# A hybrid diffusion trunk on one core: the output projection takes its weight tiles from the MLP's larger set, and the input's squares take the tiles of split weights

## The chip, the cores and the metric

One NeuronCore of one Trainium2 chip runs the whole kernel. The metric is the device time of one execution in microseconds (us). The engines are TensorE (PE, with its weight loads, PEld), VectorE (DVE), ScalarE (ACT), GpSimd (POOL) and SyncE (SP, which here only issues DMAs). Each works through its own queue in order.

## What is computed

The reference, cut down to what matters here (one layer, 512 latent positions, 256 context positions, model width 2048, MLP width 8192):

```python
mod_l = silu(c) @ w_ada + b_ada                  # 6 x 2048 values: shift, scale, gate, twice
mod_c = silu(c_ctx) @ w_ada + b_ada
p_l = modulate(rms_norm(x, g_mix), sh1_l, sc1_l) @ w_in
p_c = modulate(rms_norm(ctx, g_mix), sh1_c, sc1_c) @ w_in
f_l = fourier_mix(p_l[..., :512], w_fourier)
y_l = ssd_mixer(p_c[..., 512:], p_l[..., 512:], ...)
x = x + gt1_l * (concat([f_l, y_l]) @ w_out)     # the output projection
x = x + gt2_l * (square(relu(modulate(rms_norm(x, g_mlp), sh2_l, sc2_l) @ w_mlp1)) @ w_mlp2)
return rms_norm(x, g_final)
```

## The kernel before

Everything is float32 and lies transposed: channels on the 128 partitions, positions along the free axis, 16 tiles of 128 channels for a width of 2048. Most products split both operands into two parts, `hi` (rounded to the fp32r type by ACT) and `lo` (the remainder, by DVE), and add three matmuls (`mm3`, L106 to L109). `load_split` (L92) loads one weight tile of up to 128 x 1024 through the SP queue into a raw tile `wraw`, makes `whi` on ACT (L100) and `wlo` on DVE (L101), all inside `tc.high_priority()`.

The tiles come from pools with a fixed number of buffers per name. The set that the first half uses (opened at L228) has 3 raw tiles (`wp`) and 2 of each split tile (`ws`). A second set, for the MLP, is opened at L761 with 7 raw tiles and 3 of each split tile; the dictionary `pools` says which set is in use. Instructions are put in order at compile time by a planner: each engine's queue is filled by priority and by the planner's own idea of when inputs and buffers are ready, and this order is fixed when the kernel runs. An instruction that waits holds all that stand behind it in its engine's queue.

**The start.** `spread` (L176) loads the condition vector, one row at a time, into an `araw` tile and spreads it over the partitions by matmuls on `ones` (L183); there is one for the latent condition `cl` and, after the norm of the input, one for the context condition `ccl`. The input `xr` comes in eight loads of two channel tiles each (L317). Its squares (L322, ACT, 128 x 1024 each) go into eight `araw` tiles and are added up by DVE (L324); two matmuls (L328) sum over the channels, and `rstd_of` makes the inverse root (L154 to L159). `araw` has 5 buffers. The same 5 take the 512 KB tiles of `w_ada` (`ada_half`, L169), from which DVE makes the modulation by one multiply-and-sum for each (L173). The first 16 steps of the input projection (L335 to L353) each need four such sums: DVE forms `xr * rstd` (L344), ACT modulates it (`mtmp`, L345), and PE makes eight fp32 products (L349).

**The output projection.** Column block j of 16 has its weights in `w_o[j]`, 1 MB. For j = 0 to 2 the products over the first 13 channel tiles stand ahead of the last SSD results (L743 to L751), and the last three follow in the loop (L797, 192 KB each). From j = 3 on `product` (L111) makes a block of two `load_split` of 512 KB, 24 matmuls of 512 columns each. The sum `ps` (one of 3 `acc` banks) is gated and added to the input tile `x2` by DVE (L803), stored to DRAM by a POOL DMA (L804) and squared for the next norm (L784, L785). `background(3)` puts three `ada_half` steps behind each block: 48 loads of 512 KB for the modulation of the MLP.

**The entry of the MLP.** After the norm (L789, L154 to L159), x is read back, modulated and split into `chi`, `clo` (L837 to L861), and the first MLP weights `w_1s` are loaded by `load_split` in 16 tiles of 384 KB (L848).

Of the kernel before, what the change touches and what calls it, by code (L numbers as in the profile page):

```python
# [7 lines left out]
F32 = mybir.dt.float32  # L8
F32R = mybir.dt.float32r
AF = mybir.ActivationFunctionType  # L10
# [4 lines left out]
P = 128  # L15
D = 2048
KT = D // P
L = 512
# [11 lines left out]
HALF = 1024  # L30
# [25 lines left out]
def tile_hybrid_trunk(ctx, tc, xT, ctxT, cvec, ccol, vec, alog, w_ada, w_adr, w_ins, w_zs, w_in, w_dt, w_f, w_o,  # L56
                      w_1s, w_1, w_2, cst, sel_d, dft, cw_d, out):
    nc = tc.nc
    v = nc.vector
    s = nc.scalar  # L60
    te = nc.tensor
# [7 lines left out]
    pools = {}  # L69
# [5 lines left out]
    def acc(n=L):  # L75
        return psa.tile([P, L], F32, name="acc")[:, :n]

    def bank():
        return psb.tile([P, 512], F32, name="bank")
# [12 lines left out]
    def load_split(src, n, b=None):  # L92

        with tc.high_priority():
            raw = raw_tile()[:, :n]
            hi = pools["ws"].tile([P, HALF], F32R, name="whi")[:, :n]
            lo = pools["ws"].tile([P, HALF], F32R, name="wlo")[:, :n]
            rv = raw if b is None else raw.rearrange("p (a b) -> p a b", b=b)
            nc.sync.dma_start(out=rv, in_=src)
            s.copy(hi, raw)  # L100
            v.tensor_sub(lo, raw, hi.bitcast(F32))  # L101
        if b is None:
            return hi, lo
        return hi.rearrange("p (a b) -> p a b", b=b), lo.rearrange("p (a b) -> p a b", b=b)

    def mm3(ps, a, b, first, last, on=False):  # L106
        te.matmul(ps, a[0], b[0], start=first, stop=False, skip_group_check=on)  # L107
        te.matmul(ps, a[1], b[0], start=False, stop=False, skip_group_check=on)  # L108
        te.matmul(ps, a[0], b[1], start=False, stop=last, skip_group_check=on)  # L109

    def product(ps, src, x, cuts=(8, 16)):  # L111
        k0 = 0
        nk = len(x)
        for k1 in cuts:
            w = load_split(src[:, k0:k1], (k1 - k0) * src.shape[2], src.shape[2])
            for k in range(k0, k1):
                mm3(ps, (w[0][:, k - k0], w[1][:, k - k0]), x[k], k == 0, k == nk - 1)
            k0 = k1
# [8 lines left out]
    ones = const.tile([P, P], F32, name="ones")  # L127
# [99 lines left out]
    w_stack = ExitStack()  # L227
# [3 lines left out]
    ara = ada_stack.enter_context(tc.tile_pool(name="ara", bufs=5))  # L231
# [47 lines left out]
    def background(n):  # L279
        for _ in range(min(n, len(todo))):  # L280
            todo.pop(0)()
# [16 lines left out]
    with tc.tile_pool(name="st", bufs=1, side="right") as st, tc.tile_pool(name="st2", bufs=2, side="right") as st2, \  # L298
            tc.tile_pool(name="st4", bufs=3, side="right") as st4:
        cl = st.tile([P, 2 * HALF], F32, name="cl")  # L300
        xr = st.tile([P, KT, L], F32, name="xr")
# [14 lines left out]
            sl = slice(h * 2, h * 2 + 2)  # L316
            nc.sync.dma_start(out=xr[:, sl], in_=xT[:, sl])  # L317
        s.activation(cs, cs, AF.Silu)
        qs = None
        for h in range(8):  # L320
            q = ara.tile([P, HALF], F32, name="araw")
            s.activation(q, xr[:, h * 2:h * 2 + 2].rearrange("p a b -> p (a b)"), AF.Square)  # L322
            if qs is not None:
                v.tensor_add(q, qs, q)  # L324
            qs = q
        ps = bank()
        for h in range(2):
            te.matmul(ps, ones, qs[:, h * L:(h + 1) * L], start=h == 0, stop=h == 1)  # L328
        rstd = st.tile([P, L], F32, name="rstd")
        rstd_of(rstd, ps, L, 1.0 / D, st2, ("sq", "sr"))  # L330
        spread(ccl, 1)
# [221 lines left out]
    ps = acc(LC)[:48]  # L553
    product(ps, w_dt, cm)
    dt_finish(ps, LC, NCH, cp, ("cxs", "cx_tok"))
    for g in range(NG):
        b_tok = cp.tile([P, NCC, P], F32, name="cb_tok")
        x_tok = cp.tile([P, NCC, HG * 64], F32, name="cx_tok")
        for i in range(4):
            t = T_B + g if i == 0 else T_X + g * 3 + i - 1  # L560
            ps = acc(LC)
# [5 lines left out]
        for d in range(2):  # L567
# [8 lines left out]
            h = cp.tile([P, HG, 64], F32, name="ch")  # L576
# [166 lines left out]
    for j in range(3):  # L743
        ps = acc()
# [14 lines left out]
    new = {}  # L759
# [19 lines left out]
    def sumsq(accum, x, pool, k):  # L779
        if k == 0:  # L780
            s.activation(accum, x, AF.Square)
        else:
            q = pool.tile([P, L], F32, name="nq")
            s.activation(q, x, AF.Square)  # L784
            v.tensor_add(accum, accum, q)  # L785
# [6 lines left out]
    for j in range(KT):  # L792
        x2 = g2p.tile([P, L], F32, name="x2")
        nc.sync.dma_start(out=x2, in_=xT[:, j])
        if j < 3:
            ps = first[j]
            w = load_split(w_o[j][:, 13:16], 3 * P, P)  # L797
            for k in range(13, KT):
                mm3(ps, (w[0][:, k - 13], w[1][:, k - 13]), cat[k], False, k == KT - 1)
        else:  # L800
            ps = acc()
            product(ps, w_o[j], cat)
        v.scalar_tensor_tensor(x2, ps, mod[:, 32 + j:33 + j], x2, ALU.mult, ALU.add)  # L803
        nc.gpsimd.dma_start(out=x2_d[j], in_=x2)  # L804
        sumsq(a1, x2, xp2, j)
        background((21 - NSB) // 2)
    v.scalar_tensor_tensor(s1, mod[:, 64:80], 1.0, vt[:, V_GMLP:V_GMLP + KT], ALU.add, ALU.mult)
    g2_stack.close()
    w_stack.close()
    big_stack.close()  # L810
    pools.update(new)

# [17 lines left out]
    for p in range(8):  # L832
        i, q = p // QC, p % QC
        xa = pr.tile([P, 8, LC], F32, name="xa")
        for k, sl in ((p + 8, slice(1, 3)), (p, slice(0, 4, 3))):
            x = xp2.tile([P, L], F32, name="nt")
# [88 lines left out]
    for rr in range(N1P, NP):  # L925
        ct = stg.tile([P, 4, LC], F32, name="ct")
        sn = stg.tile([P, 4, LC], F32, name="sn")
        ps = {}
# [100 lines left out]
    for c in range(NFC):  # L1029
# [15 lines left out]
        for op in range(4):  # L1045
# [53 lines left out]
            for o in range(2):  # L1099
                for i in range(2):  # L1100
                    j = 2 * op + o + 8 * i
# [9 lines left out]
    ps = bank()  # L1111
# [94 lines left out]
```

## Time and profile before

| what | value |
|---|---|
| median of 3 runs | 2326.96 us (2325.39 to 2330.8) |
| the profiled execution's own time | 2328.78 us |
| its span, first to last instruction | 2327.0 us |
| PE busy | 2235.5 us, 96% of the span |
| DVE busy | 1902.4 us, 82% |
| mean granted TensorE clock | 0.988 of full speed |
| moved by DMA | 499.33 MB |

The profiled execution is one more execution, 1.8 us above the median. In the views, L12 is line 12 of the kernel before. A row of the timeline gives start, duration, engine, line, operation, output<-input and, in brackets, how long the engine had been idle and what ended it. A row of the windows gives, for each engine, busy time (and instructions), then the granted TensorE clock, the mean busy share of the 16 DMA engines and GB/s. Matmuls are pipelined, so their busy times overlap and starts are the better measure.

### The profile page before, as it was taken

How to read it: one execution, taken by the hardware profiler on the slowest of the kernel's cores; microseconds unless marked ns; L12 is line 12 of the kernel's file. 1: busy time of each engine (PE TensorE's matmuls, PEld its weight loads, DVE VectorE, ACT ScalarE, POOL GpSimd, SP SyncE). 2: the span in 40 equal slices, each digit the busy share in tenths (PEclk: the TensorE clock that was granted, in tenths of full speed). 3: DMA queues.
4: the chain of work that ended last, by engine and by line, in shares of the span. 5: the costliest groups of instructions: out<-in, count | busy, mean ns of one | idle time of the engine just before them, and what ended most of it. 6: DMA issues, size and time to landing. Idle time of an engine off the chain costs nothing.

```text
span 2327.0 us, 38787 instructions
## 1 busy us (share of the span) xinstructions
PE 2235.5 (96%) x15218; PEld 1992.7 (86%) x15218; DVE 1902.4 (82%) x2615; ACT 1190.4 (51%) x1706; POOL 319.7 (14%) x346
## 2 busy tenths in 40 slices
PE   6999999999999999799999999999999999999996
PEld 2347779877777777699999999999999999999996
DVE  7977879988889767677888887777997897788788
ACT  4135235456666522255455555555765666566554
POOL 0000000000001000111122121111122222222210
PEclk9999999999999999999999999999999999999998
DMA  7988967743324599546555554344899999999983
GB/s 291 336 313 279 334 235 262 266 145 111 98 88 141 180 316 317 182 136 208 174 180 185 179 167 130 124 131 136 240 265 269 268 255 256 270 268 231 245 261 109
DMA packets 150942, 499.33 MB, mean 215 GB/s; under 512 B 17780, under 2 KB 18692, under 8 KB 150504
## 3 DMA queue, kind: packets, MB, share of 16 engines
q1 hardware_dynamic: 111464, 387.39, 49.1%
q0 software_dynamic: 38144, 107.38, 20.4%
q8 instruction: 119, 1.95, 0.3%
q10 hardware_dynamic: 1152, 2.10, 0.2%
q14 instruction: 63, 0.52, 0.1%
HBM read 433.87 MB, written 62.92 MB: 213 GB/s over the span
## 4 chain that ended last, share of the span: by engine, by line
PE 66%; DVE 15%; DMA 12%; issue 4%; ACT 2%; SPq 0%; POOL 0%; DVEq 0%; ACTq 0%; POOLq 0%
PE acc L108 10%; PE acc L109 10%; PE acc L107 10%; PE bank L107 8%; PE bank L108 8%; PE bank L109 8%; DMA araw<-in_w_ada_dram 3%; DVE wlo L86 2%; DVE araw L173 2%; DMA wraw<-in_w_dram 2%; DVE wlo L101 2%; DMA araw<-in_w_adr_dram 2%; DMA wraw<-in_w_adr_dram 1%; PE bank L349 1%; DVE adacc L201 1%
## 5 line engine op out<-in xcount | busy, mean ns | idle before, releaser
L86 DVE TENSOR_TENSOR wlo<-wraw,whi 128x1024 fp32r<-128x1024 f32 x427 | 552.1, 1301 | 161.1 <-ACT whi L85 158.1
L85 ACT CAST whi<-wraw 128x1024 fp32r<-128x1024 f32 x427 | 444.9, 1048 | 440.0 <-PE bank L109 167.9
L107 PE MATMUL bank<-chi,whi 128*128 128x256 f32 (+1 forms) x2000 | 570.4, 285 | 4.4 <-DVE x2f L1094 2.5
L108 PE MATMUL bank<-chi,wlo 128*128 128x256 f32 (+1 forms) x2000 | 570.2, 285 | 2.5 <-DVE wlo L86 2.5
L109 PE MATMUL bank<-clo,whi 128*128 128x256 f32 (+1 forms) x2000 | 569.8, 285 | 0.0
L107 PE MATMUL acc<-chi,whi 128*128 128x256 f32 (+1 forms) x1512 | 430.9, 286 | 6.7 <-ACT chi L843 6.7
L108 PE MATMUL acc<-chi,wlo 128*128 128x256 f32 (+1 forms) x1512 | 432.8, 286 | 4.6 <-DVE wlo L86 4.3
L109 PE MATMUL acc<-clo,whi 128*128 128x256 f32 (+1 forms) x1512 | 431.0, 285 | 0.0
L107 PEld LDWEIGHTS bank<-chi,whi 128*128 128x128 f32 x2000 | 385.3, 193 | 6.0 <-DVE x2f L1094 2.7
L108 PEld LDWEIGHTS bank<-chi,wlo 128*128 128x128 f32 x2000 | 385.4, 193 | 3.9 <-DVE wlo L86 2.9
L109 PEld LDWEIGHTS bank<-clo,whi 128*128 128x128 f32 x2000 | 385.3, 193 | 1.0
L107 PEld LDWEIGHTS acc<-chi,whi 128*128 128x128 f32 x1512 | 290.0, 192 | 9.2 <-ACT chi L843 7.5
L108 PEld LDWEIGHTS acc<-chi,wlo 128*128 128x128 f32 x1512 | 290.4, 192 | 8.4 <-DVE wlo L86 6.8
L108 PE MATMUL acc<-bh,wlo 128*128 128x512 f32 x720 | 285.8, 397 | 9.9 <-DVE wlo L101 9.9
L109 PEld LDWEIGHTS acc<-clo,whi 128*128 128x128 f32 x1512 | 290.3, 192 | 1.7 <-DVE clo L845 0.6
L107 PE MATMUL acc<-bh,whi 128*128 128x512 f32 x720 | 285.8, 397 | 5.7 <-DVE x L803 3.1
L109 PE MATMUL acc<-bl,whi 128*128 128x512 f32 x720 | 285.0, 396 | 0.0
L100 ACT CAST whi<-wraw 128x1024 fp32r<-128x1024 f32 (+3 forms) x145 | 142.8, 987 | 241.3 <-PE acc L109 207.4
L101 DVE TENSOR_TENSOR wlo<-wraw,whi 128x1024 fp32r<-128x1024 f32 (+3 forms) x145 | 165.7, 1145 | 34.3 <-ACT whi L100 34.0
L108 PEld LDWEIGHTS acc<-bh,wlo 128*128 128x128 f32 x720 | 136.3, 189 | 43.7 <-DVE wlo L101 15.8
L107 PEld LDWEIGHTS acc<-bh,whi 128*128 128x128 f32 x720 | 136.4, 189 | 35.5 <-issue 4.4
L109 PEld LDWEIGHTS acc<-bl,whi 128*128 128x128 f32 x720 | 136.4, 189 | 28.6 <-issue 1.0
(349 smaller groups left out, 3329.7 us busy)
## 6 DMA issues: line engine op xcount, KB each, us to landing
wraw<-in_w_dram SPq DMA_DIRECT2D x276, 512.0 KB, 4.8
araw<-in_w_ada_dram SPq DMA_DIRECT2D x164, 512.0 KB, 6.8
wraw<-in_w_in_dram SPq DMA_DIRECT2D x84, 512.0 KB, 4.5
wraw<-in_w_dram POOLq DMA_DIRECT2D x64, 512.0 KB, 8.0
x<-ca POOLq DMA_DIRECT2D x112, 256.0 KB, 8.2
araw<-in_w_adr_dram SPq DMA_DIRECT2D x48, 512.0 KB, 4.4
wraw<-in_w_adr_dram SPq DMA_DIRECT2D x32, 512.0 KB, 3.9
hid<-ct POOLq DMA_DIRECT2D x32, 512.0 KB, 5.0
```

The costliest lines, as they stand in the source:

```text
L85: s.copy(hi, raw)
L86: v.tensor_sub(lo, raw, hi.bitcast(F32))
L100: s.copy(hi, raw)
L101: v.tensor_sub(lo, raw, hi.bitcast(F32))
L107: te.matmul(ps, a[0], b[0], start=first, stop=False, skip_group_check=on)
L108: te.matmul(ps, a[1], b[0], start=False, stop=False, skip_group_check=on)
L109: te.matmul(ps, a[0], b[1], start=False, stop=last, skip_group_check=on)
L173: v.tensor_tensor_reduce(o, a, cond[:, hf * HALF:(hf + 1) * HALF], 1.0, last if hf else first, ALU.mult, ALU.add, dst[:, ch:ch + 1] if hf ...
L201: v.scalar_tensor_tensor(a, w[:, j], cs[:, k:k + 1], a, ALU.mult, ALU.add)
L349: te.matmul(a[:n], w[:, o:o + n], tmp, start=k == 0, stop=k == KT - 1)
```

## The change

At the start the squares of the input leave the `araw` tiles. They are made in four pairs in the tiles `whi` and `wlo` of the first weight set (2 buffers each): ACT squares the first of a pair, DVE multiplies the second with itself and adds the two, and PE sums each pair by two matmuls at once, so that there are eight matmuls in one sum where there were two. In the output projection the first weight set is closed at j = 3, not behind the loop, and `pools` is switched to the MLP's set there, so that the 26 `load_split` of the blocks j = 3 to 15 take the 7 raw and 3 split tiles.

```diff
-        qs = None
-        for h in range(8):
-            q = ara.tile([P, HALF], F32, name="araw")
-            s.activation(q, xr[:, h * 2:h * 2 + 2].rearrange("p a b -> p (a b)"), AF.Square)
-            if qs is not None:
-                v.tensor_add(q, qs, q)
-            qs = q
         ps = bank()
-        for h in range(2):
-            te.matmul(ps, ones, qs[:, h * L:(h + 1) * L], start=h == 0, stop=h == 1)
+        for h in range(0, 8, 2):
+            q = [pools["ws"].tile([P, HALF], F32R, name=n).bitcast(F32) for n in ("whi", "wlo")]
+            x = [xr[:, i * 2:i * 2 + 2].rearrange("p a b -> p (a b)") for i in (h, h + 1)]
+            s.activation(q[0], x[0], AF.Square)
+            v.tensor_mul(q[1], x[1], x[1])
+            v.tensor_add(q[0], q[0], q[1])
+            for j in range(2):
+                te.matmul(ps, ones, q[0][:, j * L:(j + 1) * L], start=h == 0 and j == 0, stop=h == 6 and j == 1)
...
         else:
+            if j == 3:
+                w_stack.close()
+                pools.update(new)
             ps = acc()
             product(ps, w_o[j], cat)
...
     g2_stack.close()
-    w_stack.close()
     big_stack.close()
-    pools.update(new)
```

## Rows read from the trace of the kernel before

**Rows 1.** The page: busy time of each engine.

```profile
PE 2235.5 (96%) x15218; PEld 1992.7 (86%) x15218; DVE 1902.4 (82%) x2615; ACT 1190.4 (51%) x1706; POOL 319.7 (14%) x346
```

**Rows 2.** Windows, the start of the kernel.

```profile
18.00:20.00 2.00, 0.05 (x1) 0.05 (x1) 1.79 (x2) 0.00 (x0) 0.00 (x0) 1.00 0.12 31
...
40.00:95.00 55.00, 53.93 (x120) 20.00 (x118) 55.00 (x100) 9.64 (x14) 0.00 (x0) 1.00 0.92 327
```

**Rows 3.** Timeline, 0 to 45 us, in order of start.

```profile
3.05 7.16 PE L183 MATMUL bank<-araw,ones 1*128 1x512 f32 x8 [3.05 <-DMA araw<-in_cvec_dram]
...
10.12 1.22 DVE L324 TENSOR_TENSOR araw<-araw 128x1024 f32<-128x1024 f32 x1 [9.11 <-ACT araw L322]
...
10.75 5.78 ACT L322 ACTIVATE araw<-xr 128x1024 f32<-128x1024 f32 x6
...
18.59 12.42 SPq L169 DMA_DIRECT2D araw<-in_w_ada_dram  x8
...
19.95 3.78 PE L328 MATMUL bank<-araw,ones 128*128 128x512 f32 x4 [9.73 <-DVE araw L324]
...
23.66 4.03 PE L183 MATMUL bank<-araw,ones 1*128 1x512 f32 x8
...
28.77 0.69 DVE L159 SCALAR_TENSOR_TENSOR rstd<-sr,rstd 128x512 f32<-128x512 f32 x1
...
32.59 0.08 DVE L173 DVE_READ_ACCUMULATOR2_ANT mod<- 128x1 f32 x1
...
33.57 5.04 PE L349 MATMUL acc<-mtmp,wraw 128*128 128x512 f32 x6 [5.88 <-ACT mtmp L345]
```

**Rows 4.** Timeline of PE, input projection: the first matmuls of four steps.

```profile
80.09 2.84 PE L349 MATMUL acc<-mtmp,wraw 128*128 128x512 f32 x6 [0.45 <-ACT mtmp L345]
...
88.00 2.84 PE L349 MATMUL acc<-mtmp,wraw 128*128 128x512 f32 x6 [0.45 <-ACT mtmp L345]
...
103.20 2.77 PE L349 MATMUL acc<-mtmp,wraw 128*128 128x512 f32 x6
...
110.43 2.77 PE L349 MATMUL acc<-mtmp,wraw 128*128 128x512 f32 x6
```

**Rows 5.** Windows, output projection.

```profile
805.00:810.00 5.00, 1.91 (x7) 1.16 (x6) 4.45 (x7) 3.22 (x5) 0.00 (x0) 0.94 1.03 413
810.00:815.00 5.00, 5.00 (x18) 3.89 (x17) 3.21 (x5) 1.91 (x3) 0.55 (x1) 0.72 0.89 291
...
830.00:835.00 5.00, 5.00 (x17) 3.93 (x16) 2.30 (x4) 0.00 (x0) 0.00 (x0) 0.67 0.88 272
...
830.00:950.00 120.00, 112.82 (x480) 90.04 (x479) 87.45 (x124) 26.94 (x31) 5.93 (x11) 0.99 0.92 316
...
957.00:972.00 15.00, 14.46 (x63) 11.31 (x61) 5.87 (x10) 1.68 (x2) 0.54 (x1) 1.00 0.05 19
```

**Rows 6.** Waits of PE, 797 to 979 us (total, times, longest).

```profile
PE acc L108 <- DVE wlo L101: 8.0, 10, 2.8
PE acc L107 <- DVE x L803: 3.1, 1, 3.1
PE acc L107 <- ACT whi L100: 2.5, 1, 2.5
```

**Rows 7.** DMA issues, 797 to 830 us (KB each, median us to landing).

```profile
wraw<-in_w_1s_dram SPq DMA_DIRECT2D x10, 384.0 KB, 7.5
```

**Rows 8.** Timelines of ACT and of DVE, head of the output projection.

```profile
805.63 3.25 ACT L100 CAST whi<-wraw 128x768 fp32r<-128x768 f32 x5 [5.23 <-DMA wraw<-in_w_1s_dram]
...
806.49 3.63 DVE L101 TENSOR_TENSOR wlo<-wraw,whi 128x768 fp32r<-128x768 f32 x5 [0.55 <-ACT whi L100]
```

**Rows 9.** Timelines of DVE and PE, end of the output projection.

```profile
971.73 0.75 DVE L803 SCALAR_TENSOR_TENSOR x<-acc,mod,x 128x512 f32<-128x512 f32 x1 [8.51 <-PE acc L109]
...
981.75 0.80 PE L107 MATMUL acc<-chi,whi 128*128 128x512 f32 x1 [6.69 <-ACT chi L843]
```

**Rows 10.** Windows, entry of the MLP.

```profile
982.00:1020.00 38.00, 38.00 (x225) 33.70 (x226) 37.59 (x63) 26.37 (x38) 6.01 (x11) 0.94 0.52 161
```

## The prediction

> **What bounds the kernel now.** I read the page first: PE is busy for 96% of the span, so time can only come from places where PE waits or runs at a low clock [rows 1]. I then took windows and timeline of the two stages that the edits touch. In both the DMA share is 0.92 over long stretches [rows 2, 5]. For the output projection I added the waits of PE and the DMA issues.
>
> In the start PE does nearly nothing until its first product of the input projection at 33.57 us; from there it is almost never idle. That product waits for `mtmp`, and `mtmp` waits for the fourth sum over `w_ada` (L173, done at 32.67), though the norm was ready at 28.77 + 0.69 = 29.46 [rows 3]. The sums are late because the loads of `w_ada` are first issued at 18.59, when the squares leave `araw` tiles; between 18 and 20 us DMA runs at 0.12 [rows 2, 3]. Later, from 40 to 95 us, DVE is busy for all of 55 us and PE's steps come 7.91 us apart (80.09 to 88.00), where later, with DVE ahead, they come 7.23 apart (103.20 to 110.43) [rows 2, 4].
>
> In the output projection PE has an average of 112.82 / 480 = 0.235 us for a matmul, so a half block of 24 is worth 5.6 us and a block 11.3 us; DMA moves 316 GB/s at a share of 0.92 [rows 5]. Between 797 and 972 us PE waits 8.0 us for `wlo`, 3.1 for L803 to empty a bank and 2.5 for `whi` [rows 6]. After the two longer gaps the granted clock reads 0.72 and 0.67 in five-microsecond windows, stretches that mix the 1.2 GHz level with 2.4 GHz, which cost 5 x 0.28 + 5 x 0.33 = 3.0 us [rows 5]. All of it together, 13.6 + 3.0 = 16.6 us, is the most that this stage can give. Part of the cause stands in rows 7: ten loads of `w_1s`, which nobody needs before 981 us, go out before 830 us, because the MLP's tiles stand empty and the loads have high priority. They are 10 x 0.393 = 3.93 MB, 12.4 us at 316 GB/s, in a stage whose DMA is nearly full, while from 957 to 972 us DMA lies at 0.05 [rows 5, 7]. ACT's and DVE's casts of them stand in front of those that PE waits for: ACT waits 5.23 us for their DMA [rows 8].
>
> **The change, part by part. The start.** Removed: four of eight squares on ACT and three of seven adds. Added on DVE: four multiplies and, for seven adds, four: eight operations of 1.22 us, 9.8 us, in place of 8.5 [rows 3]; DVE has nothing else before 25 us, so this is hidden by its idle time, and would cost 1.3 us if DVE had the sums to do then. Added on PE: six matmuls, twelve passes. A pass took 7.16 / 8 = 0.895 to 3.78 / 4 = 0.945 us before 24 us, and 0.50 as a mean of the eight from 23.66 [rows 3].
>
> When is the sum of squares ready? The last square ran until 16.53, so the last part of x was there at about 15.5; one multiply and one add give 17.9, two matmuls at the slow pace 21.7, against 23.73 now, so 2 us earlier. But two split tiles of a name make a ring: the third pair waits until PE has read the first, and PE is with the spread of `cl` until 10.2. Sixteen passes from there at 0.895 end at 24.5, 0.8 later than now; at 0.50 for the last pairs it would be near 19.8, 3.9 earlier. And if the planner puts the eight matmuls of the second spread, whose rows no longer wait for `araw`, ahead of the last pairs, it is up to 7.2 later. I take no change of the norm (it lies between the ring and the free chain), with ends of -3.9 and +8.0.
>
> The Trainium skill, "TensorE: Matmul & The Clock Gate", Part 1, has the throttled clock as the default, which activity releases. By it the added matmuls would bring the fast pace earlier and the norm 3.9 us earlier; the eight matmuls from 3.05 to 10.2 us, slow to the last, do not bear that out.
>
> What does come earlier is `w_ada`: `araw` is free while x lands, so about three loads go out behind x and two more follow as the rows of the spread leave. Their sums fall into DVE's idle time and no longer hold `mtmp`. Then the first product follows the norm by the multiply L344 and `mtmp`; the latter took 0.9 us from 32.67 to 33.57, the former is an operation of the 0.69 us of L159, and with latencies I estimate 1.9 us: 31.3 instead of 33.57, -2.3 us. DVE also enters the long stretch some five sums ahead, so that the 7.91 - 7.23 = 0.7 us lost in each of some four steps go: 2.7 at most, of which I take -2.2. Sum of the start: -4.5. Bounds: -3.9 - 2.3 - 2.2 = -8.4, and +8.0 - 2.3 = +5.7 with nothing won in the steps.
>
> **The output projection.** The 26 tiles of blocks 3 to 15 now come before `w_1s` in the ring of seven. So `w_1s` can't be loaded ahead of the stage; in its place at the head go seven half blocks that the stage needs anyway. A `w_1s` load waits until a tile that lies seven before it has been split, which puts the first near nine half blocks, 50 us, before PE's end and the last of seven near 17. PE can be three split tiles deep instead of two: DVE may be 11 us late, not 5.6, before PE waits. With blocks of 2 x 0.524 MB of weights, 3 x 0.524 of `w_ada`, 0.26 in and 0.26 out, 3.15 MB in 11.3 us, PE asks for 279 GB/s, less than the 316 that DMA gave, so PE should be the limit. I count 7.0 of the 8.0 us for `wlo`, the 3.1 for L803 and 2.4 of the 3.0 of clock as won: -12.5. The 2.5 us at the head stay, since the first half blocks take the place that `w_1s` has in the queues of SP, ACT and DVE, with 512 KB instead of 384. Bounds: -16.6, all of it; and, if DMA decides by bytes alone, only the three loads of `w_1s` beyond the seven leave the stage: 1.18 MB, -3.7. Closing the first set issues nothing.
>
> **The entry of the MLP.** Now three tiles of `w_1s` are split by 810 us. After the change two are by the end of PE's work, and the third is made beside the norm. Between 982 and 1020 us DVE is busy 37.59 of 38 us [rows 10], so a split that falls there is paid in full: the five in rows 8, three of 768 columns and two of 384, take 3.63 us, so 0.9 for 768. One is +1; all three are +2.7. Their loads are hidden behind the 10 us from 971.73 to 981.75 in which PE waits for the norm and `chi` [rows 9].
>
> Sum: -4.5 - 12.5 + 1.0 = -16.0 us, from 2328.78 to 2312.8. The median of the runs is 1.8 below the profiled time, so I state 2311. What can't be told from no change is 0.2%, 4.7 us.
>
> **The rivals.** (1) Forecast, both edits pay: 2311, own range 2302 to 2318. Chance 0.52.
>
> (2) DMA is the limit in the output projection. For it: share 0.92, and DVE's waits for `w_ada` are what makes `wlo` late. Against it: 279 below 316 GB/s. Then -3.7 - 4.5 + 1 = -7.2: 2320. Chance 0.18.
>
> (3) The ring of two split tiles and the second spread make the norm late: the start at +5.7, the rest as forecast: -5.8, 2321. For it: slow passes until 24 us. Against: the second spread has lower priority. Chance 0.12.
>
> (4) Nothing much: waits change their names, DVE's order is still paced by `w_ada` landing: 2325 to 2329. Chance 0.10.
>
> (5) Slower: the burst at the head. Seven loads of 512 KB, 3.67 MB, are 8.9 us at the 413 GB/s of 805 to 810 us [rows 5]; if the 192 KB tiles of blocks 1 and 2 and the `x` tiles of L794 stand behind all of them on SP, PE's wait of 2.5 us grows by 6.4, that for L803 by as much, and with DMA the limit only 3.7 comes back: +12.8 - 3.7 + 2.7 - 4.5 = +7.3, 2334. It decides once the head loses more than 3.7 - 2.7 + 4.5 + 4.7 = 10 us. For it: `w_1s` in the same place held ACT for 5.23 us [rows 8]. Against: the first 192 KB tiles need no new set and go first. Chance 0.08. The Trainium skill, "DMA: Bandwidth & Descriptors", Queues, rings and completion order, says that descriptors of one row are consumed in ring order, so what SP issues later waits for the burst; by that rule this rival gets its full price.
>
> **The numbers.** Faster 0.80 (1, 2 and nearly all of 3), same 0.12, slower 0.08. The range leaves out rival 5, most of 4 and a little below the forecast: 2302 to 2326.
>
> **What would show it.** First L173 before 20 us and first L349 near 31; steps 7.2 us apart from the second on. No `w_1s` load before 900 us; PE's wait for `wlo` under 2 us; L803 of the last block near 955 instead of 971.73, with the norm and `chi` some 10 us behind it as now. Wrong, if DMA stays full to the end of the stage, if PE's first wait grows past 10 us, or if the eight matmuls end after 25 us.

## The result and the profile after

The kernel after takes 2312.35 us in the median of 5 runs (2309.25 to 2319.66), the kernel before on the same chip 2330.8 us (2325.39 to 2335.89). The ratio is 0.9935, with an interval of 0.9918 to 0.9951: 11 to 19 us less, where 16 were forecast. The profiled execution took 2314.14 us, its span is 2312.4 us against 2327.0. One execution, of the run with the switch at j = 4, took 3169.61 us at a mean granted clock of 0.637 and is left out of that run's ratio.

In the page, PE's busy time has hardly moved [rows 1], so over the whole span the 14.6 us came out of PE's idle time (91.5 us before, 75.1 after). From here on L12 is line 12 of the kernel that a view belongs to: L803 of the kernel before is L805 in the kernel after.

```profile
PE 2237.3 (97%) x15230; PEld 1993.4 (86%) x15230; DVE 1902.7 (82%) x2616; ACT 1189.8 (51%) x1706; POOL 318.8 (14%) x346
```

The start, in the timeline of PE (compare [rows 3]). L327 are the matmuls on the squares, L183 those of the two spreads, L348 is the first product of the input projection:

```profile
10.03 5.50 PE L327 MATMUL bank<-whi,ones 128*128 128x512 f32 x8
...
16.22 1.99 PE L327 MATMUL bank<-whi,ones 128*128 128x512 f32 x4 [0.69 <-DVE whi L325]
18.13 1.98 PE L183 MATMUL bank<-araw,ones 1*128 1x512 f32 x4
20.04 1.99 PE L327 MATMUL bank<-whi,ones 128*128 128x512 f32 x4
...
31.49 5.49 PE L348 MATMUL acc<-mtmp,wraw 128*128 128x512 f32 x6 [7.55 <-ACT mtmp L344]
```

And of DVE: the first sum over `w_ada`, and the end of the norm.

```profile
18.55 1.28 DVE L173 CUSTOM_DVE_ANT_0 araw<-araw,cl,vt 128x1024 f32<-128x1024 f32 x1
...
28.09 0.69 DVE L159 SCALAR_TENSOR_TENSOR rstd<-sr,rstd 128x512 f32<-128x512 f32 x1
```

The first product comes 2.1 us sooner, the sixteenth step starts at 143.37 in place of 146.61, 3.2 us sooner.

The output projection. The stage is measured here from the matmuls on `qa` (L708), which stand ahead of it on PE, to the last gate by DVE (L805). In that stretch PE has the same 717 matmuls before and after. Windows of the kernel after (columns as in [rows 5]): the whole stage, then its head.

```profile
785.13:959.60 174.47, 167.89 (x717) 136.08 (x717) 121.09 (x170) 43.01 (x54) 8.65 (x16) 0.98 0.85 299
...
805.00:810.00 5.00, 3.88 (x9) 2.71 (x9) 5.00 (x8) 2.74 (x5) 0.00 (x0) 0.56 1.02 419
810.00:815.00 5.00, 5.00 (x18) 4.04 (x17) 0.19 (x1) 0.63 (x1) 0.54 (x1) 0.76 1.03 409
815.00:820.00 5.00, 5.00 (x23) 4.13 (x22) 0.00 (x0) 0.87 (x1) 0.00 (x0) 1.00 0.58 234
820.00:825.00 5.00, 5.00 (x23) 4.13 (x22) 4.09 (x6) 1.25 (x3) 0.54 (x1) 1.00 0.44 98
```

Before, the same stretch (787.55 to 971.73) is 184.18 us long, 170.49 of it busy. The stage lost 9.7 us: 7.1 of PE's idle time (13.7 to 6.6) and 2.6 of its busy time. Waits of PE in the stage after (total, times, longest; compare [rows 6]):

```profile
PE acc L107 <- ACT whi L100: 3.3, 2, 2.7
PE acc L108 <- DVE wlo L101: 3.2, 4, 1.6
```

The wait for L803 is gone, that for `wlo` fell from 8.0 to 3.2, that for `whi` grew from 2.5 to 3.3. Behind it stands ACT: the total of its waits for PE to give back a `whi` tile fell from 54.2 us (18 times, 785 to 960 us) to

```profile
ACT whi L100 <- PE acc L109: 16.7, 5, 8.3
```

What makes the `whi` wait at the head stands in the timeline of ACT:

```profile
803.98 3.77 ACT L100 CAST whi<-wraw 128x1024 fp32r<-128x1024 f32 x5 [6.00 <-DVE half L173]
```

These five casts are of 1024, 384, 1024, 384 and 1024 columns in this order: the first 512 KB tile of block 3, whose load was issued at 795.78, stands in ACT's queue ahead of the two 192 KB tiles of blocks 1 and 2, whose loads had been issued at 791.04 and 794.37. PE waits for these two (805.49 and 806.85, shown further down). The view names DVE for the 6.00 us, but the 512 KB load landed at 803.90, and in the run with the switch at j = 4, where the same cast waits 6.11 us, it names the load. In the kernel before a cast of `w_1s` stands in that place [rows 8].

The first `w_1s` load, in the timeline of SP, and the end of the stage, in those of DVE and PE (compare [rows 7, 9]):

```profile
918.53 0.33 SPq L99 DMA_DIRECT2D wraw<-in_w_1s_dram  x1
...
959.60 0.75 DVE L805 SCALAR_TENSOR_TENSOR x<-acc,mod,x 128x512 f32<-128x512 f32 x1 [3.57 <-PE acc L109]
...
970.56 0.80 PE L107 MATMUL acc<-chi,whi 128*128 128x512 f32 x1 [6.68 <-ACT chi L843]
```

The entry of the MLP takes 10.96 us instead of 10.02. The books of the two profiled spans: -3.2 to the sixteenth step, +0.8 from there to `qa`, -9.7 in the stage, +0.9 in the entry, -3.4 from the first MLP product to the end, sum -14.6. The two stretches that neither edit touches are not repeatable to better than this: over the twelve profiles of this study the one from the sixteenth step to `qa` is between 639.6 and 649.3 us, the last between 1336.6 and 1345.3, and the kernel before happens to have the longest of the latter. So the +0.8 and the -3.4 are not put down to the change; what the edits touch makes -12.0 of the -14.6.

### The profile page after: what moved, and what is told of

Same layout as the page of the kernel before. It is cut to its first block, busy times and chain, and to the rows that moved or that the text cites. A ratio compares the mean times of both kernels' runs of the same rounds, so it can differ in the third digit from the quotient of the medians.

```text
span 2312.4 us, 38807 instructions
## 1 busy us (share of the span) xinstructions
PE 2237.3 (97%) x15230; PEld 1993.4 (86%) x15230; DVE 1902.7 (82%) x2616; ACT 1189.8 (51%) x1706; POOL 318.8 (14%) x346
## 4 chain that ended last, share of the span: by engine, by line
PE 62%; DMA 16%; DVE 15%; issue 4%; ACT 3%; SPq 0%; POOL 0%; DVEq 0%; ACTq 0%; POOLq 0%
PE acc L108 10%; PE acc L109 10%; PE acc L107 10%; PE bank L107 8%; PE bank L109 8%; PE bank L108 8%; DMA araw<-in_w_ada_dram 5%; DMA wraw<-in_w_dram 5%; DVE araw L173 4%; DVE wlo L86 2%; DVE wlo L101 2%; DMA araw<-in_w_adr_dram 2%; PE bank L676 1%; PE bank L691 1%; PE bank L641 1%
## 5 line engine op out<-in xcount | busy, mean ns | idle before, releaser
L107 PEld LDWEIGHTS acc<-chi,whi 128*128 128x128 f32 x1512 | 290.7, 193 | 10.1 <-ACT chi L843 8.1
```

## The experiments

All ratios are to the kernel before on the same chip. "Stage" is the stretch from `qa` to the last gate, always the same 717 matmuls; sets are raw/split tiles from the fourth output tile on (in the last row from the fifth). Stage and times are from one profile each. The four kernels with a stage like that of the kernel after (after, output projection only, squares in araw, Silu behind Exp) have it between 173.49 and 174.68 us, the two with that of the kernel before between 184.18 and 184.95, so a difference of about 1 us between stages is not shown.

| kernel | set | first w_1s load | first product | 16th step | stage | PE idle in it | ratio (interval) |
|---|---|---|---|---|---|---|---|
| before | 3/2 | 798 us | 33.57 | 146.61 | 184.18 | 13.7 | 1 |
| after | 7/3 | 919 | 31.49 | 143.37 | 174.47 | 6.6 | 0.9935 (0.9918 to 0.9951) |
| squares only | 3/2 | 799 | 31.47 | 143.35 | 184.95 | 13.4 | 0.9981 (0.9964 to 0.9997) |
| output projection only | 7/3 | 921 | 33.37 | 146.90 | 173.49 | 5.0 | 0.9947 (0.9929 to 0.9966) |
| raw tiles only | 7/2 | 924 | 31.38 | 143.24 | 183.40 | 14.5 | 0.9962 (0.9947 to 0.9977) |
| w_1s behind | 3/2 | 949 | 31.38 | 143.81 | 177.90 | 9.0 | 0.9961 (0.9949 to 0.9972) |
| split tiles only | 3/3 | 799 | 32.04 | 143.94 | 176.23 | 10.1 | 0.9945 (0.9933 to 0.9957) |
| squares in araw | 7/3 | 921 | 31.36 | 143.15 | 174.68 | 5.9 | 0.9940 (0.9927 to 0.9954) |
| Silu behind Exp | 7/3 | 923 | 30.55 | 143.92 | 173.58 | 6.3 | 0.9927 (0.9914 to 0.9940) |
| w_ada on POOL | 7/3 | 927 | 31.65 | 143.53 | 187.53 | 16.8 | 0.9982 (0.9971 to 0.9993) |
| split, w_1s behind | 3/3 | 936 | 31.57 | 143.50 | 173.48 | 6.8 | 0.9923 (0.9910 to 0.9936) |
| switch at j = 4 | 7/3 | 915 | 32.11 | 143.98 | 173.18 | 5.4 | 0.9923 (0.9909 to 0.9937) |

### Each edit alone

The squares alone: the kernel before with the first hunk of the change and nothing else. The output projection alone is the kernel after with the squares as before:

```diff
-        for h in range(0, 8, 2):
-            q = [pools["ws"].tile([P, HALF], F32R, name=n).bitcast(F32) for n in ("whi", "wlo")]
...
+        for h in range(8):
+            q = ara.tile([P, HALF], F32, name="araw")
```

> Only the first edit (squares in the tiles of split weights); the output projection as before. If the two edits add up, the start gives what the trace of the changed kernel shows for it: first product of the input projection near 31.5 us instead of 33.57, last step of it near 143.4 instead of 146.6, some 2.4 us left at 794 us, and the output projection takes 175 to 176 us from the load of clb to the last L803, as before (795.98 to 971.73). Total 2 to 4 us less than before, ratio 0.998 to 0.999. Rival: the start's lead is used up later (in a wait that stands at a fixed time), and the ratio is 1.000; or the start is worth more than the trace says, and most of the 0.9935 is here.

> Only the second edit (output projection from block 3 on with the MLP's tile set); the squares as before. If the edits add up, the stretch from the load of clb to the last L803 takes 166 us instead of 175.75, the entry of the MLP (last L803 to first product of the MLP) 11.0 instead of 10.0, and the total is 8 to 12 us less than before, ratio 0.995 to 0.9965. Rival: the second edit pays only with DMA already ahead from the first; then the stretch stays above 172 us and the ratio above 0.998.

The squares alone have the start of the kernel after and the stage of the kernel before, and the output projection alone the reverse. 0.9981 x 0.9947 = 0.9928, the kernel after has 0.9935: the two edits add, as far as the intervals tell. By the ratios the squares are worth 4.4 us of 2330 (0.7 to 8.4), the output projection 12.3 (7.9 to 16.5).

### Which part of the new set pays

The seven raw tiles alone, with the split tiles of the old set until after the loop:

```diff
             if j == 3:
-                w_stack.close()
-                pools.update(new)
+                pools["wp"] = new["wp"]
```

> The changed kernel, but at block 3 only the raw tiles change to the MLP's set (7); the split tiles stay at 2 until the loop ends. Theory A: what pays is that w_1s no longer goes out at the head (its loads and its casts on ACT and DVE); here w_1s is out of the head too, so the stretch from clb to the last L803 stays at 166 to 168 us. Theory B: what pays is the third split tile (PE may be 11 us ahead of DVE, not 5.6); then PE's wait for wlo is back at 6 to 8 us and the stretch is 171 us or more. Closing the old set after the loop may also delay nothing.

The old set to the end, with the `w_1s` loads put behind the last `w_o` load in SP's order, so that they leave the head of the stage:

```diff
-            nc.sync.dma_start(out=rv, in_=src)
+            dma = nc.sync.dma_start(out=rv, in_=src)
+            if gate_w.get("hold"):
+                issue_behind(dma, gate_w["last"])
...
-            if j == 3:
-                w_stack.close()
-                pools.update(new)
...
+    gate_w["hold"] = True
```

`hold` is set behind the loop, and until then `last` is the last load issued.

> The changed squares, the output projection with the old set of 3 raw and 2 split tiles throughout, and each load of w_1s ordered on SP behind the last load of w_o. Theory A (w_1s at the head is the cost): the stretch from clb to the last L803 falls to 166 to 169 us with the old tiles; the entry of the MLP may lose 1 to 3 us because all of w_1s comes late. Theory B (more tiles are what pays): the stretch stays at 172 us or more.

The three split tiles alone:

```diff
             if j == 3:
-                w_stack.close()
-                pools.update(new)
+                pools["ws"] = new["ws"]
```

> The kernel after, but from the fourth output tile on only the split pool is the new one (three tiles of each half); the raw tiles stay the old three, and the old set is closed after the loop. Theory B (the third split tile is what pays, and the first w_1s loads being late takes the queue out of the head): as long as the kernel after, ratio to the kernel before 0.993 to 0.9955, stage from the clb load to the last L804 166 to 168.5 us, PE waits for wlo under 5 us in it, no w_1s load before 900 us. Rival (the seven raw tiles are what lets the loads run ahead): the stage takes 170 us or more, and the waits for wlo are 8 us or more, as in the run with the raw tiles alone turned round.

Against the 184.95 us of the squares alone, the third split tile by itself takes 8.7 us off the stage and the order of `w_1s` by itself 7.1; the seven raw tiles, which put `w_1s` back as well, only 1.6. From the load of `clb` to the last gate, the stretch of the expectations, the three take 167.80, 169.45 and 174.95 us (175.75 before, 166.03 after): theory B for the raw tiles, nearly theory A for `w_1s`, and for the split tiles the theory by the time but the rival by the `wlo` waits (8.5 us). The ratios are too coarse for this: raw tiles alone (0.9962) and `w_1s` behind (0.9961) can't be told apart by them, so that the ranking of these two rests on one profile each. One expectation for the split tiles was wrong in its premise: with the old raw tiles `w_1s` finds the MLP's seven raw tiles empty and is loaded from 798.63 on, as before. So its row tells the split tile by itself, and it still gets most of the way. Waits of PE in the stage, all that there are, with the seven raw tiles alone, and then with the split tiles alone:

```profile
PE acc L108 <- DVE wlo L101: 14.3, 11, 2.5
```

```profile
PE acc L108 <- DVE wlo L101: 8.5, 7, 2.8
PE acc L107 <- DVE x L804: 1.4, 1, 1.4
```

With two split tiles ACT can't begin the next `whi` until PE has ended the half block before the one in hand, however early the raw tile has landed. ACT's waits for PE say it: 50.3 us with the squares alone and 54.5 with seven raw tiles, against 7.6 with the split tiles alone. It isn't time lost by itself: with `w_1s` behind it is 67.6 us, in a stage of 177.90. With the raw tiles alone a burst of nine `w_o` loads stands ahead of the next load of `x` on SP, and DVE's L804 waits once 6.0 us for it. That this is what makes the `wlo` waits longer (14.3 against 8.9 with `w_1s` behind) is not shown: in the kernel after ten loads stand there, and its L805 waits for `x` 0.8 us in all.

### Where the start's gain comes from

The pairs of squares in `araw` tiles, as the squares were before, in place of `whi` and `wlo`:

```diff
-            q = [pools["ws"].tile([P, HALF], F32R, name=n).bitcast(F32) for n in ("whi", "wlo")]
+            q = [ara.tile([P, HALF], F32, name="araw") for _ in range(2)]
```

> The kernel after, with the square pairs in tiles of araw, as the squares were before, in place of whi and wlo. Theory (the freed araw tiles bring the first w_ada loads and so the first sums of L173 forward): the first L173 comes after 21 us again instead of 18.55, the first weight product at 33 to 34.5 us instead of 31.49, and the load of clb 2 to 3 us later than in the kernel after; ratio 0.994 to 0.9955. Rival (it is the norm that sets the first product; ScalarE's order has no Silu of the second spread between Ln and Exp here, so that the norm is ready some 3 us sooner): the first product at 28.5 to 31 us, and the start no later than in the kernel after.

The theory fell: the first L173 is back at 23.68 us, and yet the first product and the sixteenth step come as early as in the kernel after. The rival has the norm and the start right, but not its mechanism: the first product, at 31.36 us, is past its 28.5 to 31, 7.6 us behind the norm. Timeline of DVE in this run:

```profile
20.96 0.69 DVE L155 TENSOR_SCALAR sq<-bank 128x512 f32<-128x512 f32 x1 [2.91 <-ACT sr L154]
...
23.07 0.69 DVE L159 SCALAR_TENSOR_TENSOR rstd<-sr,rstd 128x512 f32<-128x512 f32 x1
23.68 1.28 DVE L173 CUSTOM_DVE_ANT_0 araw<-araw,cl,vt 128x1024 f32<-128x1024 f32 x1
```

The norm is ready at 23.76 us instead of 28.78, and the sums follow without a gap; the fourth ends at 30.46, and `mtmp` starts at 30.50. In the kernel before, L155 stands ahead of the first L173 in DVE's queue, and DVE waits 4.59 us there, until 24.48, for ACT's Ln. The squares in pairs give the norm sooner, the squares out of `araw` give the sums sooner; either fills the same hole.

Then the order of the second spread's Silus on ACT. In the kernel after one of the four stands, with two table loads, between Ln and Exp of the norm (the expectation counts three loads and more than one Silu):

```diff
-        s.activation(dst, t, AF.Exp, scale=-0.5)
+        e = s.activation(dst, t, AF.Exp, scale=-0.5)
...
-                s.activation(dst[:, h * HALF + j * L:h * HALF + (j + 1) * L], ps, AF.Silu)
+                a = s.activation(dst[:, h * HALF + j * L:h * HALF + (j + 1) * L], ps, AF.Silu)
+                if behind is not None:
+                    issue_behind(a, behind)
...
-        rstd_of(rstd, ps, L, 1.0 / D, st2, ("sq", "sr"))
-        spread(ccl, 1)
+        e = rstd_of(rstd, ps, L, 1.0 / D, st2, ("sq", "sr"))
+        spread(ccl, 1, e)
```

> The kernel after, with the second spread's Silus ordered behind the Exp of the first norm on ScalarE, so that no table load stands between its Ln and its Exp. Theory (the three table loads and Silus inside the norm cost 3 us of the first product, but VectorE's sums set the steps after it): norm ready near 25.5 us instead of 28.78, first product 28 to 29.5 us, but the second product at 39.5 to 41.5 (41.80 in the kernel after), since VectorE idled only 2.2 us between 20 and 28 us; load of clb 0 to 2.3 us sooner, ratio to before 0.9925 to 0.994. Rival 1: all of it is kept, clb 3 us sooner, ratio 0.992. Rival 2: the second spread is then late for the shared sums of the second step, nothing is won or 1 to 2 us are lost.

The table loads are gone from between Ln and Exp, and Exp starts 3.2 us sooner (22.79), but the norm is only ready at 27.77, since DVE's order now has two of the sums between its steps and waits 2.95 us ahead of L155. The first product comes 0.9 us sooner, the sixteenth step 0.6 later than in the kernel after, which is within what the table shows for kernels with one and the same start (143.24 to 143.98); the ratio, 0.9927, can't be told from 0.9935. Rival 2 comes nearest: nothing won.

One number goes with these starts: what DVE has done by 30 us. Windows 0 to 30 us of before, after, squares in araw, and Silu behind Exp (third pair of numbers: DVE):

```profile
0.00:30.00 30.00, 14.90 (x20) 5.28 (x20) 14.26 (x18) 17.39 (x22) 0.85 (x5) 0.96 0.68 248
```

```profile
0.00:30.00 30.00, 20.31 (x32) 7.23 (x32) 18.92 (x26) 19.29 (x22) 0.85 (x5) 0.96 0.82 293
```

```profile
0.00:30.00 30.00, 21.58 (x32) 7.92 (x32) 18.77 (x25) 13.83 (x18) 0.86 (x5) 0.88 0.79 293
```

```profile
0.00:30.00 30.00, 20.43 (x32) 7.31 (x32) 18.25 (x25) 14.16 (x19) 0.85 (x5) 0.96 0.79 288
```

The pairs give DVE 1.3 us more to do. What it is ahead, net of that, is 18.92 - 14.26 - 1.3 = 3.4 us, 3.2 and 2.7; the sixteenth step starts 3.2, 3.5 and 2.7 us sooner than before. Over all ten kernels with the pairs the head start lies between 2.7 and 3.4 us, and the gain at the sixteenth step is within 0.3 us of it in nine and 0.6 less in one (`w_1s` behind). From 40 to 80 us DVE is busy for at least 39.6 us in every kernel, so its head start is what counts, not which of its inputs was late.

### The head of the output projection

After the change DMA is half idle from 815 to 825 us, because a `w_o` load that waits for a raw tile (issued at 821.47) holds the `w_ada` loads behind it on SP. So those were moved to GpSimd's queue:

```diff
-        nc.sync.dma_start(out=a, in_=w_ada[...])
+        (nc.gpsimd if pool is g2p else nc.sync).dma_start(out=a, in_=w_ada[...])
```

> The kernel after, with the w_ada loads of the output projection issued on GpSimd's queue instead of SP's, so that they no longer stand behind a w_o load that waits for a tile. Theory (the 7 us of idle DMA at 814 to 821 us cost nothing on TensorE, which is busy all the time from 810 to 835; its waits come before): DMA share of 815:825 goes from 0.5 to 0.8 or more, the stage stays within 2 us of 166, ratio to before 0.992 to 0.995. Rival 1: the loads lost there come back as waits for wlo later; with them the stage falls by 3 us or more. Rival 2: w_ada's loads now run ahead without a brake and take the queues from w_o, the head waits grow and the stage takes 168 us or more.

Theory and first rival fell, the second rival held, and by more than it said: 13 us are lost. DMA is full (1.02 from 815 to 825 us), but the ten `w_o` loads issued from 785 to 812 us land after 11.6 us (median) instead of 8.1, the 192 KB ones after 10.6 instead of 7.2, and PE waits at the head of the stage for 8.6 us in all instead of 3.3:

```profile
808.13 0.79 PE L107 MATMUL acc<-bh,whi 128*128 128x512 f32 x1 [7.08 <-ACT whi L100]
...
810.48 0.79 PE L107 MATMUL acc<-bh,whi 128*128 128x512 f32 x1 [1.56 <-ACT whi L100]
```

The `wlo` waits behind it grow as well, from 3.2 to 8.1 us. So it looks as if the order on one queue was a priority, and the idle DMA its price. The Trainium skill, "DMA: Bandwidth & Descriptors", Queues, rings and completion order, says that a DMA engine takes turns between the queue rows that have work for it; the landing times of this run agree, but don't show the turns themselves. The edit also changes the kind of queue: from 785 to 812 us the profile counts 1008 packets as software_dynamic, where the kernel after has 144, and no run separates this from the lost order.

The gain without the burst at the head: three split tiles, three raw tiles and `w_1s` behind the last `w_o` load, the two diffs above together.

> The kernel after with the old three raw tiles kept to the end of the output projection, three split tiles from the fourth output tile on, and the w_1s loads ordered behind the last w_o load on SP's queue: what the edit brings, less the seven empty raw tiles at its head. Theory (the third split tile lets ScalarE split without waiting for TensorE; w_1s out of the way saves loads and casts; the burst of seven w_o loads is what makes the head wait and drops the clock): no PE wait for whi above 1 us near 803 to 806 us, granted clock 1.00 from 800 to 950 us, waits for wlo 2 to 5 us, 180 to 183 us from the matmul on qa to the first MLP product (185.43 in the kernel after), ratio to the kernel before 0.991 to 0.993. Rival 1 (with three raw tiles the loads come just in time and the waits for wlo stay at 8 us, as with the split tiles alone): 186 us, ratio 0.9935 to 0.995. Rival 2 (the loads of w_1s are now late for the MLP's first products): the entry from the last x2 to the first MLP product grows from 10.96 us to 13 or more.

The head is as the theory has it, no wait for `whi` and a clock of 1.00 in every window from 800 to 835 us. But the clock doesn't stay at 1.00 to 950 us, as the theory has it: behind a `wlo` wait of 1.81 us, from 887.23 to 891.39, the matmuls start 0.46 us apart on average instead of 0.23. The waits for `wlo` come to 6.7 us, nearer to the 8 of the first rival than to the theory, and 184.83 us from `qa` to the first MLP product (185.43 in the kernel after) lie between the two; the ratio is the theory's. The entry, 11.35 us, speaks against the second rival.

Last, the sets changed over one block later:

```diff
-            if j == 3:
+            if j == 4:
```

> The kernel after, with the sets changed over at the fifth output tile in place of the fourth (j == 4). Theory (the seven empty raw tiles at the head of the stage let seven w_o loads go out in front of w_ada and x, and TensorE waits there with nothing in hand; one block later it has work for 11 us while the burst passes): the wait for whi at the head falls below 1.5 us and the clock stays 1.00 at 800 to 815 us, with 1 to 3 us of wlo wait for block 3 on two split tiles; 182 to 184.5 us from the matmul on qa to the first MLP product, ratio 0.991 to 0.994. Rival (the burst only moves one block, and w_ada and x late behind it hold VectorE just as long): 185 to 187 us, ratio 0.9935 to 0.995.

The theory's mechanism fell: the wait for `whi` stays (2.77 us, at 804.20), and so does the low clock behind it. On ACT the cast of block 3's first 512 KB tile again stands ahead of the two 192 KB ones, at 802.69, and waits 6.11 us for its load, with the old set's tiles as with the new. The time from `qa` to the first MLP product, 183.58 us, is 1.9 below that of the kernel after and inside the theory's range, but by less waiting for `wlo` (2.0 us instead of 3.2) and a shorter entry (10.39 instead of 10.96). Both last versions have 0.9923 against 0.9935, with intervals that overlap nearly whole; neither is shown to beat the kernel after.

## Why the prediction was right

**The total.** Forecast -16.0 us, measured 0.65% of 2330.8 = 15.1 us (11 to 19) by the ratio and 14.6 in the profiled spans. Rival 1, that both edits pay, is what happened. That the totals lie so near is in part luck: in the profiles the stretches that the edits touch give -12.0, and 2.6 us come from stretches that they don't touch.

**The start, -4.5 forecast, -3.2 at the sixteenth step.** The first product was put at 31.3 and came at 31.49; the first L173 before 20 us came at 18.55. The steps were to give 2.2 us on top and gave 1.2. From the second step to the sixteenth 2.0 us were won, nearly as forecast (103.55 us before, 101.56 after): the steps 7.5 to 7.9 us apart are gone. But the first step takes 10.3 us instead of 9.5, without a wait of PE in it, and this loss the prediction doesn't have. The granted clock is down when the first product starts (0.50 from 30 to 35 us, before and after), and it comes back little sooner than before (0.74 from 35 to 40 us, 0.70 before), so that a first step that starts 2.1 us sooner runs longer at the low level:

```profile
36.77 5.20 PE L348 MATMUL bank<-mtmp,wraw 128*128 128x512 f32 x10
41.80 2.74 PE L348 MATMUL acc<-mtmp,wraw 128*128 128x512 f32 x6
```

Before, the six matmuls took 5.04 us [rows 3] and the ten behind them 4.78, after 5.49 and 5.20. And the cause was only half named: "the sums are late because the loads of `w_ada` are first issued at 18.59". With the loads issued as late as that (18.52), the squares in araw have the same gain, because the norm, which also held DVE, is then ready sooner. "No change of the norm" came out as 28.78 us against 29.46, but by effects that nearly cancel: the passes on the squares took 0.69 us each on average from 10.03 and 0.50 from 16.22, where those before took 0.945 at 19.95 [rows 3], so that the sum of squares was ready and Ln started 1.7 us sooner (22.07 for 23.77); and a Silu with two table loads between Ln and Exp put Exp 1.5 us later (25.97 for 24.48). The earlier fast pace is as the rule of the Trainium skill, "TensorE: Matmul & The Clock Gate", Part 1, that the prediction weighed (a throttled clock by default, which activity releases) would have it. With the squares in araw, where Ln starts at 20.24 and nothing stands between it and Exp, the norm is ready at 23.76, 5.7 us sooner than before and past the lower bound of -3.9.

**The output projection, -12.5 forecast, -9.7 measured.** The wait for L803 went as forecast (3.1). Of the `wlo` waits 4.8 us went, not 7.0. The `whi` wait at the head was to stay and grew by 0.8. The clock was to give 2.4 us and gave about 0.4: the spell of low clock behind L803's wait went with it, the one at the head grew. This can be read in the starts of PE. Timeline of the kernel after:

```profile
805.49 0.73 PE L107 MATMUL acc<-bh,whi 128*128 128x512 f32 x1 [2.66 <-ACT whi L100]
806.85 0.79 PE L107 MATMUL acc<-bh,whi 128*128 128x512 f32 x1 [0.63 <-ACT whi L100]
...
811.28 0.63 PE L109 MATMUL acc<-bl,whi 128*128 128x512 f32 x1
811.70 0.63 PE L107 MATMUL acc<-bh,whi 128*128 128x512 f32 x1
...
812.50 0.40 PE L109 MATMUL acc<-bl,whi 128*128 128x512 f32 x1
812.73 0.40 PE L107 MATMUL acc<-bh,whi 128*128 128x512 f32 x1
```

Behind the gap the matmuls start 0.42 us apart, which is the level of 1.2 GHz (the granted clock reads 0.56 from 805 to 810 us), and from 812.50 on 0.23 apart, that of 2.4 GHz (1.00 from 815 us). From 806.85 to 812.50 there are 13 intervals, 5.65 us where 13 x 0.23 would be 3.0: 2.7 us. In the kernel before two spells of about 8 intervals (809.41 to 812.80, 829.88 to 833.25) cost 1.6 and 1.5. The waits add up to -7.1 us, the clock to -0.4. The remaining 2.2 lies in busy time: a matmul's record runs 0.39 us while starts are 0.23 apart, so 0.16 us of each wait counts as busy, and with 6 waits instead of 12 that is 1.0; the start behind the first matmul of a wait comes 0.34 us after it instead of 0.23, eleven times before and four times after outside the spells, which is 0.8; 0.4 us is not accounted for.

The argument for the stage was right in both of its parts, by the runs with each alone: `w_1s` out of the head 7.1 us, a third split tile 8.7, together 10.5 (184.95 to 174.47), so they overlap. What it doesn't have is a price for the seven raw tiles, by which `w_1s` is kept back: with two split tiles they get 1.6 us where the order on SP gets 7.1. With three split tiles three raw tiles and the order on SP do as well (173.48).

**The entry, +1.0 forecast, +0.94 measured.**

**The rivals.** DMA as the limit (2320) fell: at the same DMA share, 0.91 to 0.92 from 835 to 950 us, PE is busy for 111.76 us of 115 instead of 107.82. The ring of two split tiles (2321) did not delay the norm. The burst at the head (2334) cost 0.8 us of `whi` wait instead of 6.4. Its condition was not met: the 192 KB loads went out ahead of the burst (791.04 and 794.37, the burst from 795.78), and what held PE was the cast of the burst's first tile, ahead of theirs on ACT. How dear the head can become shows in the run with `w_ada` on a second queue. Of the signs, two were missed: PE's wait for `wlo` is 3.2 us where under 2 was stated, and the last gate by DVE starts at 959.60 where it was to be near 955.

## What to carry to other kernels

A weight passes through a ring of raw tiles and a ring of split tiles; look which ring the splitting engine waits on before making either deeper: here a third split tile did alone most of what the whole new set did, and seven raw tiles alone 1.6 us of 185. Loads that nobody needs for 150 us should not find empty tiles and high priority at the head of a stage that is short of DMA, and moving loads to a second queue is not the remedy by itself: in the one run here that did so, the order of the first was given up and the stage took 13 us longer. Where an engine is busy without a gap later on, count what it has done by the start of that stretch; two late inputs can make the same hole, and here either way of filling it gave the whole gain.

## What was not expected of the hardware

Switching tables on ACT costs the load alone here. The timeline of ACT in the kernel after, between Ln and Exp of the norm:

```profile
20.76 1.28 ACT L154 ACT_TABLE_LOAD   x1
22.07 0.69 ACT L154 ACTIVATE sr<-bank,eps 128x512 f32<-128x512 f32 x1
22.77 1.28 ACT L184 ACT_TABLE_LOAD   x1
24.06 0.60 ACT L184 ACTIVATE ccl<-bank 128x512 f32<-128x512 f32 x1
24.68 1.28 ACT L156 ACT_TABLE_LOAD   x1
25.97 0.63 ACT L156 ACTIVATE rstd<-sr 128x512 f32<-128x512 f32 x1
```

Each load takes 1.28 us, begins at most 0.02 us after the operation ahead of it has ended, and the next operation follows within 0.03 us. The Trainium skill, "ScalarE: Activation LUTs", What ACT_TABLE_LOAD costs, has the same 1283 ns for the load but 2.66 us for a switch, with a drain of 1380 ns; no such drain shows here, and the measurement decides.

What a PE wait costs isn't its length alone. In the kernel after, 2.66 us and then 0.63 at the head of the stage were followed by the low level until 812.50, 2.7 us more; with three split tiles and `w_1s` behind, 2.19 us (to 803.86) and then 0.69 (to 806.88) in the same place were followed by none, every window from 800 to 835 us reads 1.00. In the kernel before, a single wait of 2.85 us (to 943.88) was followed by none either, the matmuls behind it start 0.23 us apart.
